# A hybrid decoder step on one core: one projection block placed earlier, and a set of row sums computed on GpSimd instead of TensorE

## The chip, the cores and the metric

The kernel runs on one core of a Trainium2 chip. A core has five engines with an instruction queue each: TensorE (PE in the profile, with PEld for its weight loads), VectorE (DVE), ScalarE (ACT), GpSimd (POOL) and SyncE (SP, which here issues all DMA transfers). Each engine works through its own queue in order and waits at semaphores for the others. The metric is device time in microseconds, the median over runs.

## The reference

One inference step of a two-layer trunk, for a prompt of 256 tokens and for 8 samples of 8 tokens, 320 tokens together, width 1024, in float32. Layer 0 mixes tokens by chunked spatial gating, layer 1 by a matrix memory (mLSTM) with 8 heads; each is followed by a gated MLP with a short causal convolution. What the change touches:

```python
# layer 0
u, v = jnp.split(gelu(x @ w_in), 2, axis=-1)
v = (v32 - mu) * rsqrt(var + EPS) * ln_g + ln_b
ws = jnp.where(mask, w_s[:, :L, :L], 0.0)
mixed = einsum('gts,bnsgd->bntgd', ws, vc) + b_s[:, :L].T[:, :, None]
y = (u * mixed) @ w_out
# layer 1, per head
qk = silu(causal_dwconv(qk_pre, conv_buf, conv_w, conv_b))
b = cumsum(f); D = b[t] - b[s] + i[s]; m_t = max(b + m, max D)
sc = (q . k) * exp(D - m_t)
num = exp(b + m - m_t) * (q . C) + sc . v
```

Since `ln_b` is added to `v` ahead of the mixing, its share of `mixed` is `ln_b` times the sum of a row of `ws`. These row sums, 8 groups of 128, are what the kernel calls `rsum`.

## The kernel before, in words

Every product of full precision is made of three matmuls in a reduced float32 format. Weights arrive by DMA as `raw` tiles of 128x1024; ACT rounds them to the high half `wh` (line 177), DVE subtracts to get the low half `wl` (line 178). Activations are kept the same way, as `xh` and `xl`. A *block* (`block`, line 214) is one column block of a weight matrix: 8 slices of the inner dimension, three matmuls each, 320 columns wide, into one PSUM tile `pm`. `take` (line 188) hands out the next weight tile and asks for the DMA of the tile four ahead and for the split of the tile one ahead; three buffers of `wh` and `wl` and four of `raw` bound how far ahead this can run. In layer 1 (`low_last`) a block makes all its matmuls with `wh` first and those with `wl` last.

The program is recorded step by step, and a scheduler then sets the order of each engine's queue; `pin` keeps PE's order as written, `issue_after` and `behind` put an instruction behind another.

*Layer 0* (`layer_a`, line 336). First the v half of the input projection: four groups of 512 columns, `group(0)` to `group(3)`, over three PSUM tiles each (`pv_a`). ACT applies the gelu, DVE collects statistics (`bn_stats`). `load_ws` (line 372) fetches the mixing weights `ws` (prompt) and `wss` (samples), and POOL multiplies them by their masks, lines 383 and 385. Then come 16 blocks for the u half (line 519). After the first of them, `row_sums` (line 387) splits `ws` on ACT and DVE, multiplies it by a matrix of ones on PE (PSUM tile `pr`, line 395) and has ACT copy the sums to `rsum`, of which every partition then holds a copy. `v_stats` (line 455) ends the statistics: POOL raises the variance to the power -1/2 (`rstd`, line 461), DVE makes `ve`. ACT normalises v with them (line 467), and from the fifth block on `mix(b)` (line 492) multiplies v by `ws` on PE (`pmix`). The bias of each block, `b2` (line 504), is `rsum` times a component of `ln_b` plus `b_s`, on DVE.

*Layer 1* (`layer_b`, line 685). Each head has six blocks: query, key, two for the value and two for the output gate. `gates` (line 718) runs the six blocks of head 0 and beside them, on rows of 8 partitions, the cumulative sums and maxima of the gates (`b`, `a`, `M`, `m`). At its end three PE transposes of `RS` give per-token columns (`pt`, line 813). `qk_epi` (line 822) turns a query or key block into `q` or `k`: scaling into `bpad` with space for the convolution, three convolution steps on `bcv`, a tanh (`bth`, kept as `S[h]["th"]`), the product `qs`, and its split, `qh` and `qhl` or `kh` and `khl`. `scores(h)` (line 866) makes `psc` from them, weights `w`, products `Pf` and their split `Ph`, `Pl`, `Ps`. `inter` and `numer` (lines 981, 991) multiply these by the state and by v, into `num`; `state_prompt` and `state_sample` (lines 1042, 1053) update the states (`pCp`, `pcs`). In the loop over heads (line 1138) the work of head h-1 that is left over from its scores lies between the blocks of head h. `norm_cols` (line 298) copies the normalising factors into the columns `rc`, which the transposed values need.

Of the kernel before, what the change touches and what calls it, by code (L numbers as in the profile page):

```python
# [9 lines left out]

F32 = mybir.dt.float32
# [5 lines left out]
P = 128  # L17
# [41 lines left out]
class Net:  # L59
# [276 lines left out]
    def layer_a(self):  # L336
        nc, tc, I, O = self.nc, self.tc, self.I, self.O
        with tc.tile_pool(name="ya", bufs=1) as yp, tc.tile_pool(name="la", bufs=1) as lp:
# [33 lines left out]
            def load_ws():  # L372
# [9 lines left out]
                with tc.issue_after(self.rc_made.ins):  # L382
                    nc.gpsimd.tensor_tensor(ws, ws, trit.unsqueeze(1).to_broadcast([P, NH, P]), op=MULT)
                    for r, c in quads:
                        nc.gpsimd.tensor_tensor(wss[r, :, c], wss[r, :, c], bdt[r].unsqueeze(1).to_broadcast([64, NH, 64]), op=MULT)

            def row_sums():
                wsh = lp.tile([P, NH, P], F32R, name="wsh")
                wsl = lp.tile([P, NH, P], F32R, name="wsl")
                with self.behind_split():  # L390
                    self.split(wsh, wsl, ws)
                for i in range(2):
                    pr = self.psa.tile([P, 512], F32, tag="pa", name="pr")
                    for w, a, z in ((wsh, True, False), (wsl, False, True)):
                        self.mm(pr, self.onesr, w[:, 4 * i:4 * i + 4, :].rearrange("p g t -> p (g t)"), a, z)
                    nc.scalar.copy(rsum[:, 4 * i:4 * i + 4, :].rearrange("p g t -> p (g t)"), pr)

            def group(q, hooks, k=0):
                if q not in vps:
# [55 lines left out]
            def v_stats():  # L455
                for r, o in ((slice(64, P), slice(0, 64)), (slice(0, 64), slice(64, P))):
                    nc.scalar.copy(sts[r, 4:, :], sts[o, :4, :])
                for t in range(3):
                    nc.vector.bn_aggr(mv[:, t, :], st[:, t] if t < 2 else sts)
                nc.vector.tensor_scalar(ve, mv[:, :, 1], EPS, None, op0=ADD)  # L460
                nc.gpsimd.tensor_tensor(rs, ve, self.mhalf.to_broadcast([P, 3]), op=ALU.pow)
                nc.vector.scalar_tensor_tensor(ve, mv[:, :, 0], -1.0, rs, op0=MULT, op1=MULT)

            def normalise(q):
                for t in range(3):
# [26 lines left out]
            def mix(b):  # L492
                g = b // 2
                pm = self.psa.tile([P, 512], F32, tag="pa", name="pmix")
                for t in range(2):
                    self.mm(pm[:, t * P:(t + 1) * P], v[:, t, b * P:(b + 1) * P], ws[:, g, :], True, True)
                if b % 2 == 0:

                    self.mm(pm[:, TP:TP + P], vs[:, g, :], wss[:, g, :], True, True)
                    ms[g] = pm[:, TP:TP + 64]  # L500
                    ms[g, 1] = pm[:, TP + 64:TP + P]
                sm = ms.pop((g, 1)) if b % 2 else ms.pop(g)
                b2 = lp.tile([P, 1, P], F32, tag="b2", name="b2", bufs=2)
                nc.vector.scalar_tensor_tensor(b2, rsum[:, g:g + 1, :], self.vec(V_LB + b), bs[:, g:g + 1, :], op0=MULT, op1=ADD)
                y = self.tp.tile([P, T], F32, tag="yf", name="y_a", bufs=2)
                lg = self.vec(V_LG + b)
                nc.vector.scalar_tensor_tensor(
                    y[:, :TP].rearrange("p (c t) -> p c t", c=2), pm[:, :TP].rearrange("p (c t) -> p c t", c=2), lg,
                    b2.to_broadcast([P, 2, P]), op0=MULT, op1=ADD)
                nc.vector.scalar_tensor_tensor(  # L510
                    y[:, TP:].rearrange("p (b t) -> p b t", b=NB), sm.rearrange("p (b t) -> p b t", b=NB), lg,
                    b2[:, :, :NS].to_broadcast([P, NB, NS]), op0=MULT, op1=ADD)
                nc.vector.tensor_tensor(y, y, us.pop(b), op=MULT)
                self.split_y(yh[:, b, :], yl[:, b, :], y)
# [4 lines left out]
            for b in range(16):  # L519
                ps = self.block(KD, self.x_rhs)  # L520
                if b == 0:
                    row_sums()
                    v_stats()
                t = lp.tile([P, T], F32, tag="ur", name="ur", bufs=2)
                nc.vector.tensor_tensor(halves(t), parity(ps[:, :T]), halves(self.rb), op=MULT)
# [159 lines left out]
    def layer_b(self):  # L685
# [5 lines left out]
        with ExitStack() as ctx:  # L691
# [26 lines left out]
            def gates(rp):  # L718
# [79 lines left out]
                raised = nc.scalar.activation(RS[32:40, 0:T], g, AF.Exp)  # L798
                nc.scalar.activation(RS[64:72, 0:TP], m[:, :TP], AF.Exp, scale=-1.0)
                shown = nc.scalar.activation(apart(RS[64:72, TP:384]), pairs(m[:, TP:]), AF.Exp, scale=-1.0)  # L800
                with tc.issue_after(shown.ins), tc.issue_after(raised.ins):
                    self.norm_cols(nc.scalar.copy)
                again = nc.vector.tensor_copy(RS[:64, T:384], RS[:64, TP:T])
                state_in(0)
# [3 lines left out]
                self.behind(S[0]["conv"], self.last_low)  # L808
                with tc.issue_after(low.ins), tc.issue_after(raised.ins), tc.issue_after(again.ins):
                    ps = self.block(KD, self.x_rhs)  # L810
                pt = self.psm.tile([P, 512], F32, tag="pm", name="pt")
                for t in range(3):
                    self.tr(pt[:, t * P:(t + 1) * P], RS[:, t * P:(t + 1) * P], self.ident)
# [310 lines left out]
            def blk():  # L1124
                return self.block(KD, self.x_rhs)
# [12 lines left out]
            for h in range(NH):  # L1138
# [1 line left out]
                if h in (1, 2):  # L1140
                    rows_in(h)
                if h:
                    qk_epi(h, 0, blk())
                    early(h, 0)
                    qk_epi(h, 1, blk())
                    inter(h - 1)
                    numer(h - 1)
                    early(h, 1)
                    ps = blk()
                    with self.behind_split():  # L1150
                        stats(h - 1)
                    v_epi(h, 0, ps)
                    state_prompt(h - 1)
                    made = state_sample(h - 1, order[0])
                    early(h, 2)
                    v_epi(h, 1, blk())
# [246 lines left out]
```

## Time and profile before

| | |
|---|---|
| median of 3 runs | 880.77 us (880.09 to 881.84) |
| the profiled execution's own time | 880.06 us |
| its span, first to last instruction | 878.4 us |
| granted TensorE clock | 1.00 |
| busy: PE, PEld | 870.6 us (99%), 853.2 us (97%) |
| busy: DVE, ACT, POOL | 674.8 us (77%), 508.1 us (58%), 130.3 us (15%) |
| DMA | 155.74 MB, 177 GB/s in the mean |

Divided by stages, in us from the start of the span: the v half of layer 0 runs to 60.3, its u half to 122.4, then the output projection of layer 0 and the first MLP to 389.7. The gates begin there; the loop over heads follows from 413.4 on, and the second MLP ends the program.

In a row of a timeline the first number is the start in us from the start of the span, the second the duration, then the engine, the line, the operation, what it writes and reads, and in brackets how long the engine stood idle before and who released it. A row that ends in x2 or more has several instructions merged, and its duration reaches from the first to the end of the last. In a list of groups the mean duration of one instruction stands behind the comma. A row of the chain has only start, duration and what. Matmuls overlap: the distance from one start to the next is what one costs, not its own duration.

### The profile page before, as it was taken

Reading aid. Unit: us, or ns where it says so; the run is one execution under the profiler, and the core shown is the slowest. Engines: PE = TensorE matmul, PEld = TensorE weight load, DVE = VectorE, ACT = ScalarE, POOL = GpSimd, SP = SyncE. Lnnn points to the kernel's source line nnn. Section 1 sums busy time; section 2 is a strip of 40 time slices with the busy share of each in tenths; the row PEclk is TensorE's granted clock in tenths of the full one; section 3 lists DMA queues with packets and bytes.
Section 4 is the critical chain, followed back from the end, with each engine's and each line's share of the span. In section 5 each row is a group of like instructions: output and inputs, shape, how many; then the busy total and the mean of one; then the engine's idle time right before and its main releaser. Section 6 shows DMA issues by size and latency. Waiting matters only on the chain.

```text
span 878.4 us, 16938 instructions
## 1 busy us (share of the span) xinstructions
PE 870.6 (99%) x6392; PEld 853.2 (97%) x6392; DVE 674.8 (77%) x1305; ACT 508.1 (58%) x920; POOL 130.3 (15%) x288
## 2 busy tenths in 40 slices
PE   9999999999999999999999999999999999999997
PEld 7889999999999999999999999999999999999997
DVE  6866986588878864559999998878998888786443
ACT  7558554455555544446868775656766555554442
POOL 3400000030000000014443222303003000000000
PEclk9999999999999999999999999999999999999999
DMA  8755645545445555554746867665664554555551
GB/s 278 220 197 165 178 145 178 169 154 173 157 157 167 165 163 156 166 177 138 251 146 217 254 216 217 200 212 166 193 222 151 168 165 151 166 163 165 155 153 60
DMA packets 54949, 155.74 MB, mean 177 GB/s; under 512 B 7460, under 2 KB 12716, under 8 KB 54868
## 3 DMA queue, kind: packets, MB, share of 16 engines
q1 hardware_dynamic: 54868, 154.67, 55.7%
q8 instruction: 50, 0.82, 0.4%
q14 instruction: 31, 0.25, 0.1%
HBM read 142.66 MB, written 11.99 MB: 176 GB/s over the span
## 4 chain that ended last, share of the span: by engine, by line
PE 96%; DVE 2%; ACT 1%; POOL 0%; issue 0%; DVEq 0%
PE pm L80 82%; PE pv_a L80 6%; PE num L80 2%; PE pmix L80 1%; PE pcs L80 1%; PE psc L80 1%; PE pCp L80 1%; PE phn L83 1%; PE pv L83 1%; PE pw L80 0%; PE pk L83 0%; DVE bcv L836 0%; DVE wl L178 0%; POOL nr L296 0%; ACT wh L177 0%
## 5 line engine op out<-in xcount | busy, mean ns | idle before, releaser
L178 DVE TENSOR_TENSOR wl<-raw,wh 128x1024 fp32r<-128x1024 f32 (+4 forms) x254 | 300.3, 1185 | 110.8 <-ACT wh L177 110.5
L177 ACT CAST wh<-raw 128x1024 fp32r<-128x1024 f32 (+4 forms) x254 | 255.5, 1006 | 216.0 <-PE pm L80 147.2
L80 PE MATMUL pm<-xh,wh 128*128 128x320 f32 x1216 | 356.3, 301 | 0.0
L80 PE MATMUL pm<-xl,wh 128*128 128x320 f32 x1216 | 354.6, 299 | 0.0
L80 PE MATMUL pm<-xh,wl 128*128 128x320 f32 x1216 | 308.9, 299 | 0.0
L80 PEld LDWEIGHTS pm<-xh,wh 128*128 128x128 f32 x1216 | 230.0, 189 | 0.6 <-issue 0.5
L80 PEld LDWEIGHTS pm<-xl,wh 128*128 128x128 f32 x1216 | 230.0, 189 | 0.1
L80 PEld LDWEIGHTS pm<-xh,wl 128*128 128x128 f32 x1216 | 212.0, 189 | 0.1
L80 PE MATMUL pm<-yh_f,wl 128*128 128x320 f32 x352 | 105.3, 299 | 0.0
L80 PE MATMUL pm<-yh_f,wh 128*128 128x320 f32 x352 | 105.3, 299 | 0.0
L80 PE MATMUL pm<-yl_f,wh 128*128 128x320 f32 x352 | 105.3, 299 | 0.0
L80 PEld LDWEIGHTS pm<-yh_f,wh 128*128 128x128 f32 x352 | 66.6, 189 | 0.0
L80 PEld LDWEIGHTS pm<-yl_f,wh 128*128 128x128 f32 x352 | 66.6, 189 | 0.0
L80 PEld LDWEIGHTS pm<-yh_f,wl 128*128 128x128 f32 x352 | 66.5, 189 | 0.0
L578 DVE SCALAR_TENSOR_TENSOR fcv<-fpad,vecs,fcv 128x336 f32<-128x336 f32 x88 | 49.2, 564 | 1.4
L580 ACT ACTIVATE fgl<-fcv 128x256 f32<-128x256 f32 x44 | 18.3, 415 | 37.3 <-DVE fcv L578 37.3
L80 PE MATMUL pm<-yh_a,wh 128*128 128x320 f32 x128 | 38.4, 300 | 0.0
L80 PE MATMUL pm<-yl_a,wh 128*128 128x320 f32 x128 | 38.3, 299 | 0.0
L80 PE MATMUL pm<-yh_a,wl 128*128 128x320 f32 x128 | 38.3, 299 | 0.0
L322 DVE TENSOR_TENSOR xT<-pm,xT 128x320 f32<-128x320 f32 x39 | 19.0, 488 | 24.4 <-PE pm L80 24.4
L80 PE MATMUL pm<-yhb,wh 128*128 128x320 f32 x128 | 35.9, 304 | 0.0
L80 PE MATMUL pm<-ylb,wh 128*128 128x320 f32 x128 | 35.5, 300 | 0.0
(274 smaller groups left out, 1262.8 us busy)
## 6 DMA issues: line engine op xcount, KB each, us to landing
raw<-in_f_up SPq DMA_DIRECT2D x88, 512.0 KB, 3.5
raw<-in_b_win SPq DMA_DIRECT2D x48, 512.0 KB, 4.4
raw<-in_f_dn SPq DMA_DIRECT2D x32, 448.0 KB, 3.4
C<-in_C SPq DMA_DIRECT2D x32, 258.0 KB, 5.7
out_Cs<-C SPq DMA_DIRECT2D x32, 258.0 KB, 4.4
raw<-in_a_win SPq DMA_DIRECT2D x16, 512.0 KB, 3.8
raw<-in_a_wo SPq DMA_DIRECT2D x16, 512.0 KB, 4.0
raw<-in_f_dn SPq DMA_DIRECT2D x16, 512.0 KB, 3.6
```

The costliest lines, as they stand in the source:

```text
L80: self.pin(self.nc.tensor.matmul(out, lhsT, rhs, start=start, stop=stop, skip_group_check=skip))
L83: self.pin(self.nc.tensor.transpose(out, in_, ident))
L177: self.last_split = self.hold(nc.scalar.copy(wh[:, :kn, :], raw[:, :kn, :]))
L178: self.last_low = nc.vector.tensor_tensor(wl[:, :kn, :], raw[:, :kn, :], wh[:, :kn, :].bitcast(F32), op=SUB)
L322: self.nc.vector.tensor_tensor(x, ps[:, :T], x, op=ADD)
L578: nc.vector.scalar_tensor_tensor(cv, pd[:, i:i + NC], self.vec(w + i * KF), cv, op0=MULT, op1=ADD)
L580: nc.scalar.activation(gl[:, :TP], cv[:, :TP], AF.Gelu_apprx_tanh)
```

## The change

Three edits.

1. The function `row_sums` and its call are gone. In `load_ws`, right behind the mask products, one GpSimd instruction, `partition_all_reduce`, sums `ws` over the 128 partitions and writes the sums to all partitions of `rsum`.
2. The bias steps `b2` of `mix` are put behind the last step of `v_stats`.
3. In `gates`, head 1's query block is run right after head 0's last block and ahead of the transposes `pt`, and its PSUM tile is kept until head 1's `qk_epi` takes it. In the loop, head 1's first value block takes the place that this leaves: it runs ahead of `inter` and `numer` of head 0 instead of behind them. And `norm_cols` is put behind the tanh of head 0's key (`S[0]["th"]`), where it stood behind two exponentials only.

```diff
-            def row_sums():
-                wsh = lp.tile([P, NH, P], F32R, name="wsh")
-                wsl = lp.tile([P, NH, P], F32R, name="wsl")
-                with self.behind_split():
-                    self.split(wsh, wsl, ws)
-                for i in range(2):
-                    pr = self.psa.tile([P, 512], F32, tag="pa", name="pr")
-                    for w, a, z in ((wsh, True, False), (wsl, False, True)):
-                        self.mm(pr, self.onesr, w[:, 4 * i:4 * i + 4, :].rearrange("p g t -> p (g t)"), a, z)
-                    nc.scalar.copy(rsum[:, 4 * i:4 * i + 4, :].rearrange("p g t -> p (g t)"), pr)
+                    nc.gpsimd.partition_all_reduce(rsum.rearrange("p g t -> p (g t)"), ws.rearrange("p g t -> p (g t)"), P, ReduceOp.add)
...
-                nc.vector.scalar_tensor_tensor(ve, mv[:, :, 0], -1.0, rs, op0=MULT, op1=MULT)
+                self.ve_made = nc.vector.scalar_tensor_tensor(ve, mv[:, :, 0], -1.0, rs, op0=MULT, op1=MULT)
...
-                nc.vector.scalar_tensor_tensor(b2, rsum[:, g:g + 1, :], self.vec(V_LB + b), bs[:, g:g + 1, :], op0=MULT, op1=ADD)
+                with tc.issue_after(self.ve_made.ins):
+                    nc.vector.scalar_tensor_tensor(b2, rsum[:, g:g + 1, :], self.vec(V_LB + b), bs[:, g:g + 1, :], op0=MULT, op1=ADD)
...
                 if b == 0:
-                    row_sums()
                     v_stats()
...
-                with tc.issue_after(shown.ins), tc.issue_after(raised.ins):
+                with tc.issue_after(shown.ins), tc.issue_after(raised.ins), tc.issue_after(S[0]["th"].ins):
                     self.norm_cols(nc.scalar.copy)
...
                 with tc.issue_after(low.ins), tc.issue_after(raised.ins), tc.issue_after(again.ins):
                     ps = self.block(KD, self.x_rhs)
+                S[1]["ps"] = self.block(KD, self.x_rhs)
                 pt = self.psm.tile([P, 512], F32, tag="pm", name="pt")
...
                 if h:
-                    qk_epi(h, 0, blk())
+                    qk_epi(h, 0, S[h].pop("ps") if h == 1 else blk())
                     early(h, 0)
                     qk_epi(h, 1, blk())
+                    if h == 1:
+                        ps = blk()
                     inter(h - 1)
                     numer(h - 1)
                     early(h, 1)
-                    ps = blk()
+                    if h > 1:
+                        ps = blk()
```

How the instructions stand. First ACT at the end of the gates, before the change. `wh_4850` is the high half of head 1's query block, `wh_4978` that of its key block.

```order
L798 ACTIVATE RS_4558<-g3_4564 8x320
L301 COPY nr_4617<-nr_4617 32x2
L304 COPY rc_4768<-nr_4617 32x3 x4
L177 CAST wh_4850<-raw_4695 128x1024
L838 ACTIVATE bth_4735<-bcv_4730 128x344
L177 CAST wh_4978<-raw_4777 128x1024
L848 COPY qs_4737<-qs_4737 128x64
L333 CAST kh_4740<-qs_4737 128x128
L1077 ACTIVATE th_o_4845<-o_b_4843 128x320
```

And with the change, the same stretch; `wh_4839` is now the query block's, `wh_4870` the key block's.

```order
L789 ACTIVATE RS_4547<-g3_4553 8x320
L178 CAST wh_4839<-raw_4684 128x1024
L178 CAST wh_4870<-raw_4766 128x1024
L830 ACTIVATE bth_4724<-bcv_4719 128x344
L302 COPY nr_4606<-nr_4606 32x2
L305 COPY rc_4757<-nr_4606 32x3 x4
L1069 ACTIVATE th_o_4834<-o_b_4832 128x320
L840 COPY qs_4726<-qs_4726 128x64
L334 CAST kh_4729<-qs_4726 128x128
```

The copies `nr` and `rc` moved from ahead of the two casts to behind the tanh, and a gate's tanh `th_o` moved from behind `kh` to ahead of it; `kh` still ends the stretch.

DVE in the same place with the change; `wl_4840` is the low half of head 1's query block, `wl_4871` that of its key block, `wl_5018` and `wl_5069` those of its value blocks.

```order
L784 TENSOR_TENSOR X_4535<-Xf_4556,X_4535 8x392
L832 SCALAR_TENSOR_TENSOR qs_4726<-bth_4724,bcv_4719 128x256
L834 SCALAR_TENSOR_TENSOR qs_4726<-bth_4724,bcv_4719 128x64
L334 TENSOR_TENSOR khl_4730<-qs_4726,kh_4729 128x128
L179 TENSOR_TENSOR wl_4840<-raw_4684,wh_4839 128x1024
L179 TENSOR_TENSOR wl_4871<-raw_4766,wh_4870 128x1024
L1067 TENSOR_TENSOR o_b_4905<-pm_4836,rb_4651 128x320
L179 TENSOR_TENSOR wl_5018<-raw_4802,wh_5017 128x1024
L820 TENSOR_TENSOR bpad2_4542<-pm_4867,rb_4651 128x256
L821 TENSOR_TENSOR bpad2_4542<-pm_4867,rb_4651 128x8x8
L179 TENSOR_TENSOR wl_5069<-raw_4837,wh_5068 128x1024
L828 SCALAR_TENSOR_TENSOR bcv_5000<-bpad2_4542,vecs_79,bcv_5000 128x344
```

Before, the order from `qs` to the third `wl` was the same, with `X` between `qs` and `khl`; the low half of the query block stood behind `khl` there too. New in this stretch are `bpad`, the fourth `wl` and `bcv`, which stood behind the steps of head 0's scores.

Last POOL in layer 0, before:

```order
L296 ISA
L296 TENSOR_TENSOR nr_418<-nw_417,mhalf_82 32x10
L383 TENSOR_TENSOR ws_a_126<-ws_a_126,trit_130 128x1024
L385 TENSOR_TENSOR wss_a_127<-wss_a_127,bdt_131 64x8x64 x2
L461 TENSOR_TENSOR rstd_a_697<-ve_a_696,mhalf_82 128x3
```

And with the change, where `ISA` without operands is the instruction that changes the set of programs that POOL has at hand (the profile calls it MODIFY_POOL_CONFIG), and `ISA` with operands is the sum:

```order
L297 TENSOR_TENSOR nr_418<-nw_417,mhalf_82 32x10
L384 TENSOR_TENSOR ws_a_126<-ws_a_126,trit_130 128x1024
L387 ISA
L387 ISA rs_a_129<-ws_a_126 128x1024
L386 ISA
L386 TENSOR_TENSOR wss_a_127<-wss_a_127,bdt_131 64x8x64 x2
L452 TENSOR_TENSOR rstd_a_698<-ve_a_697,mhalf_82 128x3
```

The products `wss` and the power `rstd` moved behind a change of programs, the sum, and a change back.

More of the change, by code (lines that the diff above doesn't have):

```diff
@@ L8 @@
 from concourse import mybir
+from concourse.bass_isa import ReduceOp
 from concourse.bass_utils import run_bass_kernel_spmd
```

## The prediction

> **What bounds the kernel now.** I read the busy shares first, then the chain of waits, then who waited for whom on TensorE (PE), then the timelines of the two stages that the change touches.
>
> ```profile
> span 878.4 us, 16938 instructions
> PE 96%; DVE 2%; ACT 1%; POOL 0%; issue 0%; DVEq 0%
> ...
> PE psc L80 <- ACT kh L333: 1.7, 1, 1.7
> ...
> 63.68 0.93 PE pr L80 x4
> ...
> 424.63 3.26 PE pm L80 x24
> ```
>
> The chain is PE for 96% of the span, so work taken from PE, or a wait of PE, counts one for one, and work of any other engine counts only where PE comes to wait for it. PE's one wait inside the program is 1.7 us, at the scores of head 0. The four row-sum matmuls `pr` stand on the chain with 0.93 us, and a block of 24 matmuls takes 3.26 us. So the most that the change can win is about 1.74 + 0.93 = 2.7 us. About 0.2%, 1.76 us, is what a measurement of this kernel can tell from no change.
>
> **The query block (gates stage).** These rows are the end of the gates: PE, then ScalarE (ACT), then VectorE (DVE).
>
> ```profile
> 404.43 0.30 PE L80 MATMUL pm<-xh,wh 128*128 128x320 f32 x1
> 406.61 1.25 PE L80 MATMUL pm<-xh,wl 128*128 128x320 f32 x8
> 407.69 0.30 PE L80 MATMUL pm<-xh,wh 128*128 128x320 f32 x1
> 411.12 0.49 PE L83 MATMUL pt<-ident,RS 128*128 128x128 f32 x3
> 413.36 0.39 PE L80 MATMUL psc<-qh,kh 128*128 128x256 f32 x1 [1.74 <-ACT kh L333]
> ...
> 409.66 0.19 ACT L301 COPY nr<-nr 32x2 f32<-32x2 f32 x1
> 410.59 1.05 ACT L177 CAST wh<-raw 128x1024 fp32r<-128x1024 f32 x1
> 411.54 0.48 ACT L838 ACTIVATE bth<-bcv 128x344 f32<-128x344 f32 x1
> 411.93 1.03 ACT L177 CAST wh<-raw 128x1024 fp32r<-128x1024 f32 x1
> 412.86 0.24 ACT L848 COPY qs<-qs 128x64 f32<-128x64 f32 x1
> 413.01 0.29 ACT L333 CAST kh<-qs 128x128 fp32r<-128x128 f32 x1
> 413.21 0.47 ACT L1077 ACTIVATE th_o<-o_b 128x320 f32<-128x320 f32 x1
> 413.58 1.03 ACT L177 CAST wh<-raw 128x1024 fp32r<-128x1024 f32 x1
> ...
> 413.33 0.29 DVE L333 TENSOR_TENSOR khl<-qs,kh 128x128 fp32r<-128x128 f32 x1
> 413.54 2.35 DVE L178 TENSOR_TENSOR wl<-raw,wh 128x1024 fp32r<-128x1024 f32 x2
> ```
>
> PE ends the transposes `pt` at 411.61 and stands until 413.36. The change puts head 1's query block (3.26 us, moved, not added) ahead of `pt`. If that block could run at once, `psc` would start at 411.12 + 3.26 + 0.49 = 414.87 and the whole 1.74 us would be gone. I don't think it can. A block of this layer has two sweeps: 16 matmuls with the high halves of the weights (404.43 to 406.61, 2.18 us), then 8 with the low halves (406.61 to 407.69, 1.08 us). For the moved block the low half is the first of the two `wl` at 413.54; on DVE it stands behind `khl`, before and after the change (the order quoted above). Before, PE wanted it late; now it is wanted at 411.12 + 2.18 = 413.30.
>
> When does it come? `khl` waits for `kh` on ACT. After the last `RS` (next start 409.66) ACT's new order is two `wh` (410.59 to 411.54, 0.95 each), `bth` (0.39 to the next start), `nr` and `rc` (409.66 to 410.59, 0.93), `th_o` (413.21 to 413.58, 0.37), `qs` (0.15), then `kh`: 409.66 + 1.90 + 0.39 + 0.93 + 0.37 + 0.15 = 413.40, against 413.01. `khl` follows 0.32 after, `wl` 0.21 after that: 413.93, and it takes about 1.2, to 415.14. So PE waits 413.30 to 415.15, sweeps 1.08, does `pt` 0.49 and starts `psc` at 416.7. That is 3.38 after the old 413.36, for 3.26 of moved work: **+0.1 us**. The wait does not go, it moves from `kh` to the moved block's low half. The bounds are -1.74 (low half in time) and +0.6 (ACT another half microsecond later).
>
> Head 1's value block moves ahead of `inter` and `numer` of head 0, so that two blocks, 6.52 us, still lie between head 0's transposes and `inter`; these two hide the chain from the scores to `Pl`, `Ps`. DVE now does head 1's first query steps inside that cover.
>
> ```profile
> 417.61 0.56 DVE L900 SCALAR_TENSOR_TENSOR Pf<-psc,w 128x384 f32<-128x384 f32 x1
> 419.22 1.10 DVE L333 TENSOR_TENSOR Pl<-Pf,Ph 128x384 fp32r<-128x384 f32 x1
> 420.77 0.30 ACT L905 CAST Ps<-Ps 64x128 fp32r<-64x128 f32 x1
> 421.90 0.42 DVE L828 TENSOR_TENSOR bpad<-pm,rb 128x256 f32<-128x256 f32 x1
> 422.13 1.08 PE L80 MATMUL num<-C,Qz 128*32 128x258 f32 x16
> ```
>
> `Ps` was ready at 421.07 and used after the 16 `inter` matmuls, at 423.2: 2.1 us to spare. After the change PE gets there 3.4 us later by the clock, and DVE has by then a `bpad` pair, one `bcv` and one `wl` more behind it, 0.42 + about 0.8 + 1.2 = 2.4 us. So I cost this at nothing; if the spare time were gone, `numer` would wait by what is over, 1 us at most. What is queued after `numer` (`pCp`, `pcs`) loses 3.26 us of lead and needs only `kgl` and `kgz`, which come with `Ps`.
>
> **The row sums.** Off PE: 0.93 us, on the chain, **-0.93**. Off ACT and DVE: the split of `ws` and the copies of `pr`, which PE did not wait for: nothing. The order of `b2` behind the value statistics (`ve`) lets `ve` start some 0.6 us earlier, beside PE: nothing. Onto GpSimd (POOL): a code switch, the sum over 128x1024, a switch back, all ahead of the two `wss` products and of `rstd`.
>
> ```profile
> 27.99 2.90 POOL L296 TENSOR_TENSOR nr<-nw,mhalf 32x10 f32<-32x10 f32 x1 [11.46 <-DVE nw L295]
> 33.53 2.38 POOL L383 TENSOR_TENSOR ws_a<-ws_a,trit 128x1024 f32<-128x1024 f32 x1 [2.65 <-DMA trit<-in_trit]
> 36.00 4.35 POOL L385 TENSOR_TENSOR wss_a<-wss_a,bdt 64x512 f32<-64x512 f32 x2
> 67.58 0.86 POOL L461 TENSOR_TENSOR rstd_a<-ve_a,mhalf 128x3 f32<-128x3 f32 x1 [27.24 <-DVE ve_a L460]
> ...
> L296 POOLq MODIFY_POOL_CONFIG  x2: 7/7/7, 16.5 to 16.5; - x2
> ...
> raw<-in_a_wv SPq DMA_DIRECT2D x11, 512.0 KB, 4.5
> ...
> 34.33 4.88 DVE L178 TENSOR_TENSOR wl<-raw,wh 128x1024 fp32r<-128x1024 f32 x2 [0.23 <-ACT wh L177]
> 41.37 1.20 DVE L178 TENSOR_TENSOR wl<-raw,wh 128x1024 fp32r<-128x1024 f32 x1
> 42.84 2.33 DVE L178 TENSOR_TENSOR wl<-raw,wh 128x1024 fp32r<-128x1024 f32 x2
> 47.08 1.23 DVE L178 TENSOR_TENSOR wl<-raw,wh 128x1024 fp32r<-128x1024 f32 x1 [1.91 <-ACT wh L177]
> ...
> 56.40 1.05 ACT L177 CAST wh<-raw 128x1024 fp32r<-128x1024 f32 x1 [2.41 <-PE pv_a L80]
> 59.81 1.04 ACT L177 CAST wh<-raw 128x1024 fp32r<-128x1024 f32 x1 [1.41 <-PE pv_a L80]
> ...
> 60.26 0.30 PE L80 MATMUL pm<-xh,wh 128*128 128x320 f32 x1
> 70.10 0.58 ACT L467 ACTIVATE v_s<-v_s,ve_a,rstd_a 128x256 f32<-128x256 f32 x1
> 77.48 0.61 PE L80 MATMUL pmix<-ws_a,v_a 128*128 128x128 f32 x4
> ```
>
> *Durations.* No row shows the switch or the sum. The switch at 16.5 was over before 27.99, where POOL waited for DVE: between 0 and 11.46 us. [...] The sum reads and writes as many elements as the `ws` product: at least 2.38. [...]
>
> [...]
>
> *As a neighbour.* This is what costs. At 34.33 two `wl` took 4.88 instead of 2.33: each stood until POOL's running product was done. [...] PE's blocks here take 3.46 (the casts at 56.40 and 59.81, released by PE), so the last five value blocks start at 42.96, 46.42, 49.88, 53.34 and 56.80, and each wants its low half five matmuls later, 1.08. Their `wl` are asked for at 40.45, 41.93 and 43.65 (the rows at 41.37 and 42.84, 0.9 earlier since `wss` is out of the way; the third waits for PE to free a buffer), at 47.08 and at 50.57. [...] I take **+0.5**, ends 0 and 4.7.
>
> [...]
>
> **Sum.** +0.1 - 0.93 + 0.5 = -0.3 against the profiled execution's 880.06, so 879.8. The median shown is 0.71 above that execution: **880.5 us**, no change that can be told. Its own range goes from 879.0 (no stall, and ACT a little earlier) to 882.4 (stall 2.4).
>
> **Rivals.** [...] *The query block fills the wait (faster).* If its low half is in time after all, -1.74 - 0.93 + 0.3 = -2.4, **878.4**. For it: 3.26 us of work for a hole of 1.74. Against: the order puts `wl` behind `khl`, and nothing ahead of `kh` was taken off ACT. [...]
>
> **Chances.** No change 0.50, sum in DVE's way 0.25, wait filled 0.18, long loop 0.04, and 0.03 for other small shifts, within 0.2%. So faster 0.18, same 0.53, slower 0.29. The range reaches to both near rivals: 878.3 to 884.0; what lies outside is the long loop and the worst stalls.
>
> **What will show it.** Right, if `pr` is gone from the chain, PE's wait for `kh` is gone, and a wait or gap of 1.5 to 2.2 us stands ahead of the low sweep of head 1's query block; if the sum takes 5 to 10 us and begins 42 to 47 us into the span, with one `wl` beside it of 3 to 9 us, and PE's value blocks lose under 1.5 us; if `rstd` still stands near 67. It is wrong if PE goes through the moved block without a gap (then faster), if a value block waits over 2.6 us (then slower), or if `rstd` or the first `pmix` waits for POOL.

## The result, and the profile after

| | before | with the change |
|---|---|---|
| median, run side by side | 882.14 us (880.09 to 887.09, 22 runs) | 879.88 us (879.40 to 881.35, 22 runs) |
| ratio of the two, 95% interval | | 0.9973 (0.9962 to 0.9984) |
| span of the profiled execution | 878.4 us | 877.8 us |

The median of the changed kernel is 0.27% lower, 0.16 to 0.38%. Its time lies 0.6 us below the predicted 880.5 and inside the range. The forecast called it no change that can be told, with 0.2% as the bound. This interval has values on both sides of that bound, so one measurement does not decide it. The medians are 2.3 us apart, the lowest runs 0.7 and the spans 0.6. So there are two questions: whether the terms of the sum were right, and where the other 1.6 us come from.

The chain of waits of the changed kernel, first at the end of the value blocks, then at the gates (start, duration, what):

```profile
60.97 16.30 PE pm L81 x120
77.27 0.67 PE pmix L81 x6
...
413.30 0.04 DVE khl L334
413.34 0.17 issue
413.51 1.23 DVE wl L179
414.74 0.04 issue
414.78 1.35 PE pm L81 x8
416.13 0.33 PE pt L84 x3
416.46 0.74 PE psc L81 x7
```

`pr` is gone: from the first block of the u half to the first `pmix` it takes 16.30 us, where before it was 77.65 - 60.42 = 17.23. The wait for `kh` is gone too, and in its place PE stands ahead of the low sweep of head 1's query block, behind `khl` and the `wl` that follows it. The list of PE's waits has the new one with 1.7 us:

```profile
PE pm L81 <- DVE wl L179: 1.7, 1, 1.7
```

The sum on GpSimd, with what DVE did beside it. The first four rows are POOL's, the others DVE's low halves (start, duration, what, and in brackets the idle time before):

```profile
34.09 2.38 POOL L384 TENSOR_TENSOR ws_a<-ws_a,trit 128x1024 f32<-128x1024 f32 x1 [3.03 <-DMA trit<-in_trit]
42.05 7.45 POOL L387 PARTITION_ALL_REDUCE rs_a<-ws_a  x1 [5.58 <-issue]
58.00 3.49 POOL L386 TENSOR_TENSOR wss_a<-wss_a,bdt 64x512 f32<-64x512 f32 x2 [8.50 <-issue]
67.66 0.90 POOL L452 TENSOR_TENSOR rstd_a<-ve_a,mhalf 128x3 f32<-128x3 f32 x1 [6.17 <-DVE ve_a L451]
...
34.52 4.18 DVE L179 TENSOR_TENSOR wl<-raw,wh 128x1024 fp32r<-128x1024 f32 x2 [0.23 <-ACT wh L178]
42.31 1.20 DVE L179 TENSOR_TENSOR wl<-raw,wh 128x1024 fp32r<-128x1024 f32 x1
44.23 5.89 DVE L179 TENSOR_TENSOR wl<-raw,wh 128x1024 fp32r<-128x1024 f32 x2 [0.72 <-ACT wh L178]
```

For the code switches the idle time in brackets stands: 5.58 us ahead of the sum and 8.50 ahead of `wss`. The sum took 7.45 us. It held one low half up: of the two that begin at 44.23 the second takes 1.2 us, so the first was done near 48.9, not at 45.4. PE took the first low half of these rows at 37.61 and the next at 41.17, and then one every 3.46 us; the one in question is the fifth, wanted at 51.5: no loss. The value blocks still end 0.55 us later than before (60.97 against 60.42). Of this 0.15 lies in the start, and the rest in the first low half of 34.52, which `ws` held up until 37.6; the sum had not begun then.

When the value blocks end differs from execution to execution of one kernel. So the comparison of parts below goes from the first matmul of the u half to PE's last row, the product `pb` at the end of the second MLP. Both are rows of PE's timelines, which have two decimals. The kernels stand in the order in which they are spoken of below.

| kernel | u half begins | last row of PE begins | from there to there | first `pmix` after |
|---|---|---|---|---|
| before | 60.26 | 872.85 | 812.59 | 17.22 |
| with the change | 60.81 | 872.33 | 811.52 | 16.30 |
| query_only | 61.04 | 873.54 | 812.50 | 17.23 |
| sums_only | 62.44 | 874.13 | 811.69 | 16.30 |
| no_sums | 61.92 | 873.47 | 811.55 | 16.30 |
| before_again | 61.07 | 875.35 | 814.28 | 17.23 |
| after_again | 61.41 | 872.97 | 811.56 | 16.30 |
| before_filled | 60.53 | 873.49 | 812.96 | 17.22 |
| filled_short | 60.98 | 873.56 | 812.58 | 17.23 |
| low_ahead | 61.45 | 871.80 | 810.35 | 16.30 |
| low_first | 60.64 | 870.66 | 810.02 | 16.30 |
| sum_twice | 61.23 | 874.72 | 813.49 | 16.74 |
| ws_pieces | 60.72 | 872.30 | 811.58 | 16.30 |
| low_first_dve | 61.00 | 871.03 | 810.03 | 16.30 |

### The profile page after: what moved, and what is told of

Read it like the earlier page. It is cut to its first block, busy times and chain, and to the rows that moved or that the text cites. A ratio compares the mean times of both kernels' runs of the same rounds, so it can differ in the third digit from the quotient of the medians.

```text
span 877.8 us, 16930 instructions
## 1 busy us (share of the span) xinstructions
PE 869.9 (99%) x6388; PEld 852.6 (97%) x6388; DVE 677.5 (77%) x1304; ACT 505.9 (58%) x917; POOL 138.1 (16%) x289
## 4 chain that ended last, share of the span: by engine, by line
PE 95%; DVE 2%; ACT 1%; DMA 0%; POOL 0%; issue 0%; ACTq 0%; DVEq 0%
PE pm L81 82%; PE pv_a L81 6%; PE num L81 2%; PE pmix L81 1%; PE pcs L81 1%; DVE wl L179 1%; PE psc L81 1%; PE pCp L81 1%; PE phn L84 1%; PE pv L84 1%; DMA xT<-in_xv 0%; ACT wh L178 0%; PE pk L84 0%; DVE bcv L828 0%; POOL nr L297 0%
## 5 line engine op out<-in xcount | busy, mean ns | idle before, releaser
L179 DVE TENSOR_TENSOR wl<-raw,wh 128x1024 fp32r<-128x1024 f32 (+4 forms) x254 | 304.3, 1200 | 106.4 <-ACT wh L178 105.6
```

Of the source, the lines that this page charges most:

```text
L179: self.last_low = nc.vector.tensor_tensor(wl[:, :kn, :], raw[:, :kn, :], wh[:, :kn, :].bitcast(F32), op=SUB)
```

## The experiments

### The two parts apart

`query_only` takes only edit 3, `sums_only` only edits 1 and 2, each as in the diff of the change.

> Only the move of head 1's query block and of the normalising columns; the row sums stay on PE. Theory (each part is worth what the sum of the prediction gave it): 0.0 to +0.2 us against the kernel before in a median, -0.1 by the two profiles (head 1's value transposes end 2.75 us later than before for 3.26 us moved ahead of them, from a start that is 0.38 early); PE waits 1.7 us for the low half of the moved block and no longer for kh; the times scatter as widely as the kernel before's (880 to 887). Rival (the block is what won the 2.3 us between the medians): -1.5 to -2.3 us, with times as close together as the changed kernel's (879.4 to 881.4).

> Only the row sums on GpSimd and the bias steps behind the value statistics; the query block stays where it was. Theory: -0.4 to -0.9 us against the kernel before (0.93 us of pr off PE, less a stall of 0 to 0.5 us in the value blocks), first pmix near 77.2 us, and PE's wait of 1.7 us for kh back in place; if the narrow scatter of the changed kernel comes from taking the two wss products and the pr matmuls out of the way of the early stage, it shows here too, and the median falls by 1.5 to 2.3 us. Rival (the block is what won): 0 to -0.3 us, and the times scatter as the kernel before's.

`no_sums` is the changed kernel with the sum left out:

```diff
-                    nc.gpsimd.partition_all_reduce(rsum.rearrange("p g t -> p (g t)"), ws.rearrange("p g t -> p (g t)"), P, ReduceOp.add)
...
                     nc.gpsimd.memset(wss[r, :, z], 0.0)
+                    nc.gpsimd.memset(rsum[r], 0.0)
```

> The changed kernel without its row sums: the sum over partitions is left out and rsum filled with zeros early on, so ln_b's share of the mixed values is missing. No switch of GpSimd's code, no sum, and the two wss products run right behind ws, near 36 us. Theory (the sum costs PE only what DVE's low halves are held up, 0 to 0.5 us): 0 to 0.5 us faster than the changed kernel, -0.9 to -1.0 in the profile against the kernel before, value blocks end near 60.4. Rival (GpSimd's sum and its two switches hide a longer delay elsewhere, or cost more in the median than in the profile): more than 1 us faster than the changed kernel. Second rival (what narrowed the scatter was that wss moved from 36 to 58 us): the times scatter here as the kernel before's do.

| | median | lowest | ratio to before, 95% |
|---|---|---|---|
| before, beside them | 881.83 (35 runs) | 880.25 | |
| query_only | 880.65 (12) | 880.27 | 0.9987 (0.9965 to 1.0010) |
| sums_only | 880.85 (12) | 879.34 | 0.9991 (0.9974 to 1.0008) |
| no_sums | 879.92 (12) | 879.08 | 0.9980 (0.9964 to 0.9995) |

By the stretch from the u half to PE's last row, the parts are worth nearly what they should be: the query block -0.09 us, the row sums -0.90, both -1.07 and -1.03 (two executions of the changed kernel), and the sum on GpSimd costs nothing behind that mark, since `no_sums` stands at 811.55, between those two. (Where the value blocks end was missed: 61.9 for 60.4 in `no_sums`, 78.7 for 77.2 at the first `pmix` of `sums_only`.) The lowest runs say the same: query block 0.0, row sums -0.9. Neither median reaches the 1.5 us of the second theory, and the ratios alone can't place either part. But the medians do not add up as the lowest runs do: `query_only` has the median 1.2 below that of the kernel before at an equal lowest run, and `sums_only` has three runs (881.82, 883.04 and 883.92) whose mean granted clock is 0.997, where its others show 0.999 or 1.0. The kernel before had 14 such runs of 35, `query_only` and `no_sums` none of 12 each. Why its value blocks ended so late in the profile of `sums_only` (62.44) its list of waits says: PE waited 1.9 us for the gelu that frees a PSUM tile. PE's wait for `kh` is back there too.

```profile
PE pv_a L81 <- ACT v_a L413: 1.9, 1, 1.9
PE psc L81 <- ACT kh L334: 1.7, 1, 1.7
```

### Both kernels once more, as experiments

The same two kernels, run like any other experiment.

> The kernel before itself, run as if it were an experiment. The six profiles so far agree from the first block of layer 0's u half on (the kernel before 800.75 us from its first pmix to its end, the changed one 800.53), and differ in when the value blocks end: 60.4 to 62.6 us. Theory (the gap of 2.3 us between the medians is mostly the scatter of that early stage, and the runs that serve as the yardstick scatter more than an experiment's runs do): a median of 880.4 to 881.0 here, 0.7 to 1.2 above the changed kernel run beside it, and the lowest run 0.7 above its lowest. Rival (the kernel before is wide by itself and the change narrows it): the median is 881.5 to 882.2, as of the yardstick runs.

> The changed kernel once more, beside the kernel before under the same conditions. Theory: median 879.6 to 880.1, lowest 879.4; 0.7 to 1.2 below the kernel before run in the same way. Rival: its narrow scatter of the first measurement (879.4 to 881.4 in 22 runs) was that day's, and here it is as wide as sums_only, 879.4 to 884.

Measured: 881.20 us (880.43 to 883.06, 11 runs) and 880.01 us (879.62 to 882.00, 11 runs); the kernel before beside them had 880.89 (880.17 to 882.92, 33 runs), ratio 1.0005 (0.9997 to 1.0014) and 0.9989 (0.9980 to 0.9998). So the kernel before is no narrower as an experiment, and the first theory's median of 881.0 at most is missed by 0.2. The gain repeats, at 0.11%: with the kernel before at 880.9 instead of 882.1, 0.9 to 1.2 us are left.

What told most was the profile of `before_again`. Its wait for `kh` is the same as in the first one, but 1.6 us behind it the matmuls take twice as long. PE's timeline, and PE's share of the windows (busy us and count by engine; the third number from the end is the granted clock):

```profile
414.18 0.39 PE L80 MATMUL psc<-qh,kh 128*128 128x256 f32 x1 [1.74 <-ACT kh L333]
415.69 1.42 PE L83 MATMUL pv<-ident,vTb 128*128 128x128 f32 x6
417.17 0.47 PE L80 MATMUL pm<-xl,wh 128*128 128x320 f32 x1
417.44 0.47 PE L80 MATMUL pm<-xh,wh 128*128 128x320 f32 x1
...
core 0: us, PE busy (x) PEld busy (x) DVE busy (x) ACT busy (x) POOL busy (x), PEclk, DMA share, GB/s
415.00:415.50 0.50, 0.50 (x7) 0.48 (x6) 0.50 (x1) 0.50 (x4) 0.50 (x2) 1.00 0.15 57
415.50:416.00 0.50, 0.50 (x6) 0.50 (x5) 0.50 (x2) 0.50 (x4) 0.14 (x1) 0.74 0.00 0
416.00:416.50 0.50, 0.50 (x5) 0.50 (x4) 0.50 (x1) 0.16 (x1) 0.26 (x1) 0.50 0.00 0
...
418.50:419.00 0.50, 0.50 (x3) 0.50 (x3) 0.50 (x1) 0.50 (x2) 0.43 (x2) 0.50 1.01 213
419.00:419.50 0.50, 0.50 (x4) 0.50 (x4) 0.44 (x3) 0.50 (x3) 0.00 (x0) 0.84 1.14 158
```

PE's granted clock was halved from 415.74 to 419.16 us (0.74 and 0.84 in the windows at the ends), for 3.4 us, at a cost of 1.7: from the first `pv` to the first `num` it took 424.63 - 415.69 = 8.94 us, 7.27 in the first profile. Over the whole span that is 0.002 of the mean clock. I count a run listed at 0.997 or less as one that had such a drop. That is argued, for no trace of such a run was kept: this profiled execution reads 0.998, and so does that of `before_filled` below, which has full clock here. Counted over all timings that list the clock of each run:

| | runs | of them at 0.997 or less |
|---|---|---|
| the kernel before | 122 | 44, median 882.30 us; the other 78: 880.94 us |
| sums_only | 12 | 3 |
| the eight kernels with the query block moved | 112 | 0 |

Of the 78 others eleven are listed at 0.998, and all of these stand at 881.8 us or more, so 44 may be too few. Five of the 44 stand at 887.9 to 889.3 with a clock of 0.993 to 0.995, which is more than one drop costs; no trace shows what they lost.

So the moved query block, which is worth 0.1 us by the stretch, also takes away a loss of 1.4 to 1.7 us that strikes the kernel before in about a third of its runs. How much of this shows in a median depends on how many runs of the kernel before are struck: the 78 others stand 0.9 to 1.1 above the changed kernel's two medians, about the steady 1.0 to 1.1 of the table. The first measurement lists no clocks for the kernel before. Of its 22 runs 13 stand at 881.8 us or more, where the struck runs of the others stand, so the part of its 2.3 us that the stretch does not give fits this drop, but is not shown to come from it.

### Filling the hole

What brings the drop on? In the kernel before, 4.31 us pass between the start of `pt` (411.12) and the first matmul of the next block, with the hole of 1.74 and short products and transposes in them. With the change a hole of 1.70 remains, but it lies inside a block, and the stretch without a block is 418.18 - 415.97 = 2.21 us. `before_filled` puts work that nobody needs into the hole:

```diff
                     self.tr(pt[:, t * P:(t + 1) * P], RS[:, t * P:(t + 1) * P], self.ident)
+                for t in range(22):
+                    self.mm(pt[:, 384:], self.onesr, self.xh[:, 0, :P], True, True)
```

> The kernel before with 22 idle matmuls (128x128, their result is read by nobody) behind the transposes pt, in the hole of 1.74 us in which PE waits for kh; they take 22 x 0.06 = 1.3 us and end before kh comes. Theory (a second run of the kernel before had PE's granted clock halved from 415.8 to 419.1 us, which cost 1.67 us; the hole ahead of it, between the transposes pt and the short products behind it, is what brings this on, in a third of all runs, which show a mean clock of 0.997; the moved query block takes that away, since none of 91 runs with it shows 0.997): no run at 0.997, no group of runs at 881.8 to 883, median 880.4 to 880.8, while the kernel before beside it keeps its third. Rival (the drop has another cause, by chance of the chip): a quarter to a third of the runs at 0.997 and 881.8 to 883.

> The kernel before with 12 idle matmuls instead of 22 in the hole ahead of the scores. One of them took 0.11 us, not 0.06, so 22 outlasted the hole by 0.5 us and hid what was to be seen; 12 take 1.3 us of the 1.74. Theory (the hole brings on the halved clock): no run at a mean clock of 0.997, no cost to PE, lowest run within 0.2 of the kernel before's, median 880.5 to 881.0, while a third of the runs of the kernel before beside it stand at 0.997 and near 882. Rival (the drop comes from somewhere else): a third of the runs at 0.997, median as the kernel before's beside it within 0.3.

```profile
411.65 2.65 PE L80 MATMUL pt<-xh,onesr 128*128 128x128 f32 x22
414.14 0.34 PE L80 MATMUL psc<-qh,kh 128*128 128x256 f32 x1
```

That is `before_filled`: 22 fillers took 2.4 us, 0.11 each where 0.06 was an estimate, and pushed `psc` back by 0.5. Its median is 881.43 (880.67 to 887.98, 12 runs; the kernel before 881.88, ratio 0.9996, 0.9977 to 1.0015), so the expected 880.4 to 880.8 was missed by the cost of the filler. `filled_short` has 12, and PE again waits for `kh`:

```profile
412.09 1.53 PE L80 MATMUL pt<-xh,onesr 128*128 128x128 f32 x12
414.07 0.38 PE L80 MATMUL psc<-qh,kh 128*128 128x256 f32 x1 [0.45 <-ACT kh L333]
```

It has 880.97 us (880.22 to 885.34, 12 runs), the kernel before beside it 881.77 (880.23 to 888.69, 17 runs; ratio 0.9990, 0.9969 to 1.0010), and no run at 0.997, where 7 of those 17 are at 0.997 or less. Of the 24 filled runs one is (887.98 us at 0.996, far above what one drop costs). So the hole has to do with it: at the kernel before's rate, 44 of 122, some nine of the 24 would have been struck. The 12 fillers cost PE nothing (812.58 us in the stretch of the table, 812.59 before). In the ratios alone, with 12 runs each, this can't be told.

What sets the drop off was not shown. In `before_again` it begins 3.79 us into the thin stretch, which runs from 411.95 (`pt`) to 416.76 (the next block). PE was busy there for 1.66 of the 3.40 us from 412.40 on, and in the first profile of the kernel before for the same 1.66 of the 3.40 from 411.60 on, where the clock stayed at 1.00. So one such stretch is followed by a drop and another is not, and no run varied the length of the stretch alone.

### The low half ahead

Is it really only the order on DVE that keeps the 1.7 us? `low_ahead` makes one swap: the split of head 0's key is recorded behind the take of head 1's query tile, and `khl` is put behind its `wl`. `low_first` does it with the products `qs` as well. In both the core of the edit is

```diff
-                low = qk_epi(0, 1, self.block(KD, self.x_rhs))
+                late = qk_epi(0, 1, self.block(KD, self.x_rhs))
...
-                with tc.issue_after(low.ins), tc.issue_after(raised.ins), tc.issue_after(again.ins):
+                with tc.issue_after(raised.ins), tc.issue_after(again.ins):
                     ps = self.block(KD, self.x_rhs)
+                self.behind(late(), self.last_low)
```

where `late()` records the last step of the key, and returns `khl` or the first `qs`.

> The changed kernel with one swap on DVE: the low half of head 1's query block stands ahead of khl instead of behind it. Theory (the wait of 1.7 us only moved, because this low half stood behind khl): DVE is idle from 412.2 to 413.3, so the low half is done near 413.4, PE waits 0.3 to 0.4 instead of 1.70 us, psc starts near 415.1, and the kernel is 1.2 to 1.4 us faster than the changed one. Rival (another wait takes its place: kh and khl, or raw data still under way): the gap goes to psc, and the gain is under 0.4 us.

> The changed kernel with the low half of head 1's query block ahead of the whole last step of head 0's key on DVE (qs, kh, khl) instead of behind it. With khl alone moved, PE still waited 0.4 us. Theory: this low half is done near 412.6, PE wants it at 413.1 and waits no more, psc starts near 414.7 (khl is in time for the third of its products, or late by up to 0.2), and the kernel is 1.5 to 1.7 us faster than the changed one, 0.2 to 0.4 faster than with khl alone moved. Rival (kh or khl is the next to be late): PE waits 0.3 to 1.0 us at psc, and nothing is won beyond khl alone.

PE in `low_ahead`, then DVE and PE in `low_first`:

```profile
414.11 1.35 PE L81 MATMUL pm<-xh,wl 128*128 128x320 f32 x8 [0.37 <-DVE wl L179]
```

```profile
411.23 1.23 DVE L179 TENSOR_TENSOR wl<-raw,wh 128x1024 fp32r<-128x1024 f32 x1
412.84 1.22 DVE L179 TENSOR_TENSOR wl<-raw,wh 128x1024 fp32r<-128x1024 f32 x1
414.38 0.28 DVE L334 TENSOR_TENSOR khl<-qs,kh 128x128 fp32r<-128x128 f32 x1
...
412.76 1.25 PE L81 MATMUL pm<-xh,wl 128*128 128x320 f32 x8
414.34 0.28 PE L81 MATMUL psc<-qhl,kh 128*128 128x256 f32 x1
414.71 0.39 PE L81 MATMUL psc<-qh,khl 128*128 128x256 f32 x1
```

`low_ahead`: 878.63 us (877.96 to 880.60, 12 runs), ratio to the kernel before 0.9961 (0.9943 to 0.9979); the wait fell from 1.70 to 0.37, and the stretch of the table by 1.17 to 1.21. `low_first`: 878.39 (877.70 to 880.33, 10 runs), ratio 0.9957 (0.9940 to 0.9974); PE goes through the moved block without a wait, and the stretch is 0.33 shorter again. What is next to be late is `khl`, 0.25 us at the third product of the scores. The wait had only moved, as the prediction says, and the order of two instructions on DVE is worth more than the whole change was in its steady part. `low_first` is 1.5 to 1.6 us below the changed kernel's two medians, though not timed beside it, and 1.50 to 1.54 in the stretch.

### The sum, and what holds DVE up

`sum_twice` makes the sum two times in a row; `ws_pieces` cuts the mask product of `ws` in four; `low_first_dve` is `low_first` with that product on DVE.

```diff
+                    for _ in range(2):
+                        twice = nc.gpsimd.partition_all_reduce(rsum.rearrange("p g t -> p (g t)"), ws.rearrange("p g t -> p (g t)"), P, ReduceOp.add)
+                with tc.issue_after(twice.ins):
                     for r, c in quads:
```

```diff
-                    nc.gpsimd.tensor_tensor(ws, ws, trit.unsqueeze(1).to_broadcast([P, NH, P]), op=MULT)
+                    for i in range(0, NH, 2):
+                        w2 = ws[:, i:i + 2, :]
+                        nc.gpsimd.tensor_tensor(w2, w2, trit.unsqueeze(1).to_broadcast([P, 2, P]), op=MULT)
```

> The changed kernel with the sum over partitions made twice in a row (the same sums twice, both ahead of the wss products): 14.9 us instead of 7.45. Theory (a running sum holds DVE's low halves up, and one sum is free only because the third low half from 44 us on is wanted 2.6 us after the sum lets it go): if DVE stays shut out over both, that low half is done near 56.4 and wanted at 51.5, so PE loses 4 to 5.5 us; if DVE gets in between the two sums, the next low half is done near 56.4 and wanted at 55.0, so PE loses 1 to 2 us. Rival (the sum does not hold DVE up, that low half waited for something else): no loss, within 0.3 us of the changed kernel, since wss then ends near 69 us and PE wants it only at 77.

> The changed kernel with GpSimd's mask product of ws, one instruction of 2.38 us over 128x1024, cut into four of 128x256. In four of six profiles the value blocks stood on a chain through a low half on DVE that lasted 3.0 to 3.4 us beside that product instead of 1.2. Theory (DVE is shut out as long as one GpSimd instruction runs, and gets in between two): that low half ends 1.0 to 1.8 us earlier, the value blocks end at 60.4 to 60.9, and the median is 0.2 to 0.5 us below the changed kernel's with less scatter. Rival (DVE is shut out for all four, or the chain is held by the cast or the gelu ahead of it): no difference over 0.2 us.

> As low_first, and the mask product of ws is made by DVE (about 1.2 us) instead of GpSimd (2.38 us, beside which a low half on DVE lasts 3.0 to 3.4 us). Theory (the lock beside that product stands on the chain of the value blocks in most runs): the low half near 35 us is done 0.6 to 1.2 us earlier, PE loses nothing in the value blocks after the first gelu, the sum starts 1 to 2 us earlier, and the median is 0.2 to 0.6 us below low_first's. Rival (DVE then waits in its queue for the mask's DMA, or the early start of the sum holds up a low half that is wanted soon): the same as low_first or slower.

`sum_twice`, POOL and DVE, and the engines' shares of a window at the start of layer 0's output projection. The last row is `ve_a` in the changed kernel, to compare with the row of `ve_a` here:

```profile
42.37 13.88 POOL L386 PARTITION_ALL_REDUCE rs_a<-ws_a  x2 [5.74 <-issue]
65.46 3.49 POOL L389 TENSOR_TENSOR wss_a<-wss_a,bdt 64x512 f32<-64x512 f32 x2 [9.20 <-issue]
69.12 0.91 POOL L454 TENSOR_TENSOR rstd_a<-ve_a,mhalf 128x3 f32<-128x3 f32 x1 [0.17 <-DVE ve_a L453]
...
44.64 5.64 DVE L179 TENSOR_TENSOR wl<-raw,wh 128x1024 fp32r<-128x1024 f32 x2 [0.97 <-ACT wh L178]
52.44 3.32 DVE L179 TENSOR_TENSOR wl<-raw,wh 128x1024 fp32r<-128x1024 f32 x1
68.13 0.84 DVE L453 TENSOR_SCALAR ve_a<-mv_a 128x3 f32<-128x3 f32 x1
...
126.00:130.00 4.00, 3.44 (x24) 2.98 (x22) 4.00 (x8) 1.95 (x3) 0.00 (x0) 1.00 0.26 79
...
67.35 0.17 DVE L451 TENSOR_SCALAR ve_a<-mv_a 128x3 f32<-128x3 f32 x1
```

All three expectations missed. The median rose to 882.14 us (880.00 to 883.60, 11 runs; the changed kernel 880.01 beside it), but not in the value blocks, which lost nothing to the sums. DVE got through twice: one low half came out at 49.1, the next at 50.3, a third at 55.8 where PE wanted it at 58.9. The loss lies further on. `wss` ran until 69.0 and held DVE up just where the variance is made: a low half took 1.58 us there instead of 1.23, and `ve_a` 0.84 instead of 0.17. These two make the 1.0 us by which `rstd` came later after the start of the u half than with one sum (7.89 against 6.85). PE lost 0.44 ahead of the first `pmix`, at a low half whose cast came late, and 1.3 at 128 to 130.5, where it waits for `yh_a` and `yl_a` while DVE is busy all the time. Behind `rstd` there is no time to spare: in the changed kernel ACT is busy for 12.00 of the 12 us from 70 to 82, and DVE for 7.24 to 8.00 of each 8 us from 82 to 122.

`ws_pieces`: 881.11 us (879.10 to 881.74, 11 runs), ratio 0.9992 (0.9983 to 1.0001). DVE did get in between the pieces:

```profile
34.46 4.81 POOL L386 TENSOR_TENSOR ws_a<-ws_a,trit 128x256 f32<-128x256 f32 x4 [2.82 <-DMA trit<-in_trit]
35.09 2.90 DVE L179 TENSOR_TENSOR wl<-raw,wh 128x1024 fp32r<-128x1024 f32 x2 [0.22 <-ACT wh L178]
```

Two low halves lasted 2.90 us, where they took 4.18 and 3.80 in the two profiles of the changed kernel, and GpSimd paid with 4.81 us instead of 2.38. The value blocks ended early in that profile (60.72), yet the median is 1.1 above the changed kernel's. Four runs stand at 879.1 to 879.8 and seven at 880.8 to 881.7, with no difference in the clock; the one profile is of the first kind, so what the others lost stays open. `low_first_dve`: 878.24 us (877.70 to 879.36, 11 runs), ratio 0.9954 (0.9938 to 0.9970), 0.15 from `low_first`, which can't be told apart. The hold-up at 35 us is gone, and the sum, which starts 2.7 us earlier than in `low_first` (39.04 against 41.70), holds up another low half instead (POOL, then DVE):

```profile
39.04 6.13 POOL L387 PARTITION_ALL_REDUCE rs_a<-ws_a  x1 [7.50 <-DVE vs_a L403]
...
40.31 4.34 DVE L179 TENSOR_TENSOR wl<-raw,wh 128x1024 fp32r<-128x1024 f32 x1
```

So the end of the value blocks, 60.3 to 62.4 us over the profiles, is not ruled by that one product. Its cause stays open; the profiles name a gelu, a low half or a weight tile in turn.

## Why the prediction was right, and where it was wrong

*What bounds the kernel*: right. PE has 95% of the chain after too, and every steady gain above came from a wait or a matmul of PE. The loss of clock is a loss of PE too, but no row of the profile of before showed it.

*The query block, +0.1*: right in its mechanism, off by 0.2. The wait moved to the low half behind `khl`, 1.70 us against 1.85. Measured alone the part is worth -0.09. PE's rows behind the wait, the first from the kernel before, the others from `query_only`:

```profile
414.27 0.43 PE L80 MATMUL pMb<-X,sel 128*128 128x392 f32 x1
...
417.16 0.49 PE L83 MATMUL pt<-ident,RS 128*128 128x128 f32 x3
417.41 0.36 PE L80 MATMUL psc<-qh,kh 128*128 128x256 f32 x1
418.21 0.42 PE L80 MATMUL pMb<-X,sel 128*128 128x392 f32 x1
```

Counted from the start of the u half, `psc` starts 356.37 us in, and 353.10 before: 3.27 later for 3.26 us of moved work, where the prediction had 3.38. It had added the whole 0.49 us of `pt`, but `psc` starts 0.25 after `pt`. The other 0.1 us is won behind that: from `psc` to `pMb` it takes 0.80 us, before 0.91, most of it at the third product, which no longer waits for `khl`. That DVE's new work fits into the cover at no cost held, for `num` starts 7.27 us after `pv` before and after.

*`pr`, -0.93*: right. 17.22 became 16.30 in every profile without it.

*The sum in DVE's way, +0.5*: wrong. The 0.5 was an estimate, as was its upper end of 4.7, and no run shows either: PE lost nothing to the sum. The sum took 7.45 us, with 5.58 ahead of it and 8.50 behind it for the switches, and `wss` was done at 61.5. It began at 42.05, right at the edge of the 42 to 47 that the prediction named. The low half that was asked for at 42.31, 0.26 us after its start, ran beside it in 1.20. The next one, at 44.23, was held up, but it was done near 48.9 and wanted at 51.5. The hold-up also ended ahead of the sum's row, where the two `wl` at 34.33 in the prediction stood until POOL's product was done. `low_first_dve` tests this: held to the end of the sum's row, 45.17, its low half would have been done near 46.4; it was done at 44.65, and PE took it at 44.71 without a wait.

*`rstd` near 67*: right, at 67.66. The 6.2 us in which POOL stood ahead of it are spare. The 9.45 from there to the first `pmix` at 77.11 are not: in `sum_twice` a delay of `rstd` by 1.0 us cost PE 1.9 to 2.0.

*The sum of the terms*: -0.3 was expected, -1.03 to -1.07 measured in the stretch of the table. Of the difference 0.2 is the query block's and 0.5 the sum's. The profiles' difference is only 0.6 because the value blocks ended 0.55 later, which no term had, and which another execution of the kernel before (61.07) shows as well.

*The chances*: the steady gain of 1.0 to 1.1 us is 0.12%, within the bound of 0.2%, in the class that had 0.53. So is the second measurement, 0.11%. The first, 0.27%, lies beyond the bound, where the forecast had put 0.18, though not by the way of the rival there. What the prediction lacked is the clock. It read a granted clock of 1.00 in the one profile of before and took it as given; three runs of before were no warning, at 880.1 to 881.8. That 880.5 came within 0.6 of the median rests on a base of 880.77, which is near the median of the runs at full clock (880.94 for the 78), and not on that of the 22 runs beside it, 882.14. The rival "The query block fills the wait", at 878.4, did not happen here. It is what `low_first` does in its mechanism: its stretch is 2.57 us shorter than before, against the rival's 2.4. That its median is 878.39 is in part chance.

*The long loop*: did not happen. The sum took 7.45 us for 128x1024.

## What to carry to other kernels

Moving a block into a hole filled it here only when its operands' preparation was moved with it: look where its low half, its cast and its DMA stand in the queues of the engines that make them, and move those too. Where PE's work thins out for some microseconds, take several profiles and the clock of every run before judging a change of a few tenths of a per cent; one profile at full clock did not show here that about a third of the runs lose it, as far as their mean clocks tell. And where a result varies early in a program, compare from a mark behind that part.

## What the runs showed of the hardware

PE's clock was halved for 3.4 us in one profile, from 1.6 us behind a hole of 1.74 us among short products on, at a cost of 1.7 us. By their mean clocks about a third of the runs of that kernel lost as much, and with work in the hole one of 24. A sum over partitions of 128x1024 on GpSimd took 6.13 us where no low half of DVE ran at its start (`sums_only`, `ws_pieces`, `low_first_dve`), and 7.25 to 7.45 where one had got in within 0.3 us of it, so each seems to hold up the other. The switch ahead of it took 5.6 to 5.8 us in six profiles and 6.79 and 7.50 in the two others (`ws_pieces`, `low_first_dve`), the one behind 8.0 to 9.2.

By the rows the sum shut DVE out only in its middle. A low half that came within 0.3 us of its start ran at full speed. One asked for 1.27 us after its start had to wait (40.31 above), and its own run of 1.2 us then began 1.7 us before the end of the sum's row; so it was in the changed kernel. There the mask product did shut DVE out to the end of its row: a low half asked for at 34.52 was done near 37.6, and the product ended at 36.47. Cut into four (`ws_pieces`, 34.46 to 39.27) it let two low halves through in 2.90 us. It stays open whether the sum shuts DVE out late and lets it in early, or its row is longer than its work.
